# Parking the weight sums of eighteen seven-product units of the down projection in HBM

## The chip, the core and the metric

The kernel runs on one core of one Trainium2 chip. Its time is the device time of one execution, in microseconds (us). Before the change the median of three runs was 1466.16 us (1465.68 to 1466.25).

## What is computed

One layer of a decoder trunk, 256 tokens of 2048 features, all in float32. An attention part with two branches is followed by a gated feed-forward network with a short convolution:

```python
def conv_ffn(h, w_up, conv_w, conv_b, w_down):
    a, b = jnp.split(h @ w_up, 2, axis=-1)                     # 2048 -> 2 x 5632
    ap = jnp.pad(a, ((0, 0), (CONV_WIDTH - 1, 0), (0, 0)))
    c = conv_b
    for j in range(CONV_WIDTH):                                # width 3
        c = c + conv_w[j] * ap[:, j:j + S]
    return (jax.nn.gelu(c, approximate=True) * b) @ w_down     # 5632 -> 2048
...
h = rms_norm(x, norm_mix_pre)
x = x + rms_norm(hybrid_mixer(h, ...), norm_mix_post)
h = rms_norm(x, norm_ffn_pre)
x = x + rms_norm(conv_ffn(h, ffn_w_up, ffn_conv_w, ffn_conv_b, ffn_w_down), norm_ffn_post)
```

The change concerns the product with `w_down`, the GELU, and the stages in which the change places new work.

## The kernel before

**How a product is made.** TensorE (PE) multiplies float32 in a rounded form, so every weight and every activation is split in a high and a low part, and a product is three matmuls: high·high, high·low, low·high (`mm3`, L175 to L177). A weight chunk is 128 rows of 1024 columns (512 KB). SyncE (SP) loads it into a raw tile (`raw_row`, `wchunk`), ScalarE (ACT) casts the high part (`whi`, L143), VectorE (DVE) subtracts it to get the low part (`wlo`, L144), and then PE uses both (`convert`). There are three raw tiles (`RAW`) and four split tiles (`RING`); two more buffers of a tag `flex` serve either as raw tiles (then five raw, four split) or as one split tile (three raw, five split). In `ffn_up` they are a split tile.

**Stages.** After the mixer come `ffn_up0` (c = 0) and `ffn_up(c)` for c = 1 to 10. Each makes 512 columns of `a` and 512 of `b` from 2 × 8 weight chunks, into the accumulators `ua` and `ub`; eight chunks are called a half stage. Results go through `evac` and `conv_cols`, where the convolution (L1083 to L1085), GELU (L1086 to L1091) and the product with `b` are made on ACT and DVE. The down projection is made in two parts, since the activations of all 5632 features don't fit: after c = 5 the first 24 blocks of 128 rows, for two column halves of 1024 (two calls of `pair_gemm`), and after c = 10 the other 20 blocks, 1024 columns by `pair_gemm` (B) and 1024 by `down`.

**Units.** `pair_gemm` works through units of two row blocks, in the order of a string. A plain unit ("p") has 24 matmuls. A seven-product unit ("s", `seven`) uses a scheme that needs seven block products in place of eight, 21 matmuls, and takes sums of blocks: of activations (`token_sums`) and of weights. For the weight sums GpSimd (POOL) loads the two row blocks, and DVE makes four subtractions of 128x512 (L232 to L235) into the tiles `ta` and `tb`; both, the odd block and half of the even one go through `convert`. `PAIR_ORDER` and `B_ORDER` hold the strings; before there are 4 + 3 + 3 units of this kind.

**Order.** `at(t, f)` puts a small task at a tick, and `tick()` is called after every weight chunk of a stage. A scheduler then puts the instructions of each engine in an order of its own; an engine runs its instructions strictly in that order, and one that waits holds all behind it. A tile that is to be reused is waited for by the next writer: a load on POOL into a tile waits until what read the tile before, a store among others, is done.

**Around the change.** At the start of `ffn_up` stand the residual sum and the norm (`resid`, `x2_norm`, `norm_row`): DVE writes a `row` per token tile (L1099), PE spreads it (`rrow`, L1101), and all activations of the stage are scaled with it. POOL stores the residual stream to HBM there (`park`, x_d).

Of the kernel before, what the change touches and what calls it, by code (L numbers as in the profile page):

```python
# [19 lines left out]
P = 128  # L20
D = 2048
# [17 lines left out]
GELU_C = math.sqrt(2.0 / math.pi)  # L39


def trunk_layer(ctx, tc, x, x_cols_in, conv_cols_in, g_mix_post, g_ffn_post, w_in, w_q, w_kv,
# [104 lines left out]
    def raw_row(src):  # L147
        i = cnt[0]
        cnt[0] += 1
        raw = ring_tile("raw", f"raw{i}", F32, in_turn("raw"))  # L150
        nc.sync.dma_start(raw, src)
        return raw
# [52 lines left out]
    def pair_gemm(name, w, k0, c0, order, act_of, s_of, kind, d, place, sums):  # L205
# [17 lines left out]

        def seven(u, last):
# [5 lines left out]
            lo_, hi_ = slice(0, 512), slice(512, 1024)  # L230
            w_ = convert(odd, 1024)
            vec.tensor_tensor(ta[:, lo_], even[:, hi_], even[:, lo_], op=ALU.subtract)  # L232
            vec.tensor_tensor(ta[:, hi_], odd[:, hi_], even[:, hi_], op=ALU.subtract)
            vec.tensor_tensor(tb[:, lo_], odd[:, hi_], ta[:, lo_], op=ALU.subtract)
            vec.tensor_tensor(tb[:, hi_], odd[:, lo_], tb[:, lo_], op=ALU.subtract)  # L235
# [15 lines left out]
            if last:  # L251
                d0, d1, d2, d3 = d() if callable(d) else d

                def first_sums():
                    act.copy(d0, q1)
                    vec.tensor_tensor(d1, d0, q6, op=ALU.add)
                    vec.tensor_tensor(d2, d1, q7, op=ALU.add)

                def more_sums():
                    vec.tensor_tensor(d3, d2, q5, op=ALU.add)  # L260
                    vec.tensor_tensor(d1, d1, q5, op=ALU.add)

                at(now[0], first_sums)
                at(now[0] + 1, more_sums)
# [3 lines left out]
        for i, kd_ in enumerate(order):  # L268
            if kd_ == "s":
                u = next(seven_of)  # L270
                seven(u, u == n - 1)
            else:
                plain(next(plain_of), i == len(order) - 1)
# [466 lines left out]
    tb[1], tb[2] = gate_pair(1)  # L740
    esg.close()
# [145 lines left out]
    b = now[0] + 26  # L887
# [190 lines left out]
    def conv_cols(k, a, b, slot):  # L1078
# [7 lines left out]
        act.activation(uu, cc, AF.Square)  # L1086
        vec.tensor_scalar(uu, uu, 0.044715, 1.0, op0=ALU.mult, op1=ALU.add)
        vec.tensor_tensor(uu, uu, cc, op=ALU.mult)
# [80 lines left out]

    def g_sums(u):  # L1170

        if u % 2 == 0:
            s_tiles.append(sb(p3, [P, D], f"s_{u // 2}", F32R, tag=f"x2_{u // 2}"))
# [45 lines left out]
    es7 = ffn_up0()  # L1219
    for c in range(1, 6):  # L1220
# [3 lines left out]
        if c == 4:  # L1224
            for u in range(4):
                at(now[0] + 3 + 3 * u, lambda u=u: g_sums(u))
        ffn_up(c, 4 * c)
# [6 lines left out]
    sevens_done = [0]  # L1234

    def down_place():
        sevens_done[0] += 1
        i = sevens_done[0]
        if i % 2:
            both = sb(p6, [P, D], f"rr{i}", tag="gp")  # L1240
            return both[:, 0:1024], both[:, 1024:2048]
        return [sb(p6, [P, 1024], f"rr{i}{n}", tag="f" + n, bufs=2) for n in "ab"]

    def f_sums():
        return [sb(p6, [P, 1024], f"t{n}{cnt[0]}", tag="f" + n, bufs=2) for n in "ab"]

    for p in range(2):
        d = [dsum[t][2 * p + j] for t in range(NT) for j in range(2)]
        c = pair_gemm(f"d{p}", w_down, 0, 1024 * p, PAIR_ORDER[p], lambda k, t: (GH(k)[:, t * P:(t + 1) * P], GL(k)[:, t * P:(t + 1) * P]),
                      lambda u: s_of[u], p, d, down_place, f_sums)  # L1250
# [7 lines left out]
    def b_sums(u):  # L1258

        if u % 2 == 0:  # L1260
            sb_tiles.append(sb(p3, [P, D], f"sb_{u // 2}", F32R, tag=f"x2_{u // 2}"))
# [3 lines left out]

    for c in range(6, 11):
        if c == 9:
            for u in range(B_ORDER.count("s")):
                at(now[0] + 10 + 4 * u, lambda u=u: b_sums(u))
# [4 lines left out]
    def z_block(acc, b, t):  # L1274
# [7 lines left out]
        vec.tensor_tensor(zo, z, gpost2[:, c0:c0 + n], op=ALU.mult)  # L1282
# [26 lines left out]
    b_done = [0]  # L1309

    def a_tiles(i, *n):
        return [sb(base, [P, 1024], f"dt{i}_{k}", tag=f"ahl{k}") for k in n]

    def b_place():
        b_done[0] += 1
        return a_tiles(b_done[0], *((0, 1) if b_done[0] % 2 else (4, 5)))
# [3 lines left out]
    def ud_tiles():  # L1320
        ud[:] = [x_[:, j * 512:(j + 1) * 512] for x_ in a_tiles(9, 4, 5) for j in range(2)]
        return ud

    def pair_end(i):
# [3 lines left out]

    c_db = pair_gemm("db", w_down, 24, 0, B_ORDER, lambda k, t: (GH(k)[:, t * P:(t + 1) * P], GL(k)[:, t * P:(t + 1) * P]),
                     lambda u: sb_of[u], 0, ud_tiles, b_place, lambda: a_tiles(20 + b_done[0], *((2, 3) if b_done[0] % 2 else (6, 7))))  # L1330
# [34 lines left out]
B_ORDER = "pppsppspsp"  # L1365
W_ORDER = "ppspspsp"
PAIR_ORDER = ("psppsppsppsp", "ppsppsppsppp")
# [74 lines left out]
```

## Time and profile before

| | |
|---|---|
| median of three runs | 1466.16 us |
| the profiled execution | 1466.82 us |
| its span | 1464.7 us |
| PE busy | 1454.3 us, 99% |
| DVE busy | 1088.9 us, 74% |
| ACT busy | 837.7 us, 57% |
| POOL busy | 70.2 us, 5% |
| moved by DMA | 287.6 MB, 196 GB/s on average |

The profiled execution is 2.1 us longer than its span, which goes from the first to the last instruction that the trace holds. PE, DVE, ACT and POOL are the engines; SP only starts transfers. A row of a timeline has start, duration, engine, line, operation, output<-inputs, and shape. In the windows, each engine's busy time is followed by its number of instructions, and the last three columns are PE's clock, the busy share of the DMA engines, and GB/s. Matmul durations overlap, so the pitch of starts is what a matmul costs.

### The profile page before, as it was taken

How to read it: one execution, taken by the hardware profiler on the slowest of the kernel's cores; microseconds unless marked ns; L12 is line 12 of the kernel's file. 1: busy time of each engine (PE TensorE's matmuls, PEld its weight loads, DVE VectorE, ACT ScalarE, POOL GpSimd, SP SyncE). 2: the span in 40 equal slices, each digit the busy share in tenths (PEclk: the TensorE clock that was granted, in tenths of full speed). 3: DMA queues.
4: the chain of work that ended last, by engine and by line, in shares of the span. 5: the costliest groups of instructions: out<-in, count | busy, mean ns of one | idle time of the engine just before them, and what ended most of it. 6: DMA issues, size and time to landing. Idle time of an engine off the chain costs nothing.

```text
span 1464.7 us, 20974 instructions
## 1 busy us (share of the span) xinstructions
PE 1454.3 (99%) x7567; PEld 1242.8 (85%) x7567; DVE 1088.9 (74%) x1925; ACT 837.7 (57%) x1382; POOL 70.2 (5%) x123
## 2 busy tenths in 40 slices
PE   9999999999999999999999999999999999999997
PEld 7888888888888888888888888888888888888886
DVE  7788896645667665768799976778786687677776
ACT  7588874544555554445666655555454565565553
POOL 0012110000000001000000000000000000000000
PEclk9999999999999999999999999999999999999999
DMA  8755376477655559755766666665656666667573
GB/s 296 216 164 168 105 261 197 160 212 199 188 159 159 165 162 337 263 186 173 235 206 179 199 188 187 191 187 185 206 192 207 201 186 191 186 196 232 163 234 136
DMA packets 147605, 287.60 MB, mean 196 GB/s; under 512 B 18428, under 2 KB 29597, under 8 KB 147373
## 3 DMA queue, kind: packets, MB, share of 16 engines
q1 hardware_dynamic: 137824, 252.60, 56.2%
q0 software_dynamic: 9584, 33.61, 7.3%
q8 instruction: 59, 0.97, 0.3%
q14 instruction: 46, 0.37, 0.1%
q10 hardware_dynamic: 92, 0.05, 0.0%
HBM read 277.79 MB, written 8.44 MB: 195 GB/s over the span
## 4 chain that ended last, share of the span: by engine, by line
PE 94%; DVE 2%; issue 2%; ACT 1%; DMA 1%; POOL 0%; DVEq 0%; ACTq 0%; POOLq 0%
PE accg L175 12%; PE accg L177 12%; PE accg L176 12%; PE ua L1185 10%; PE ub L1185 10%; PE ua L1189 5%; PE ub L1189 5%; PE cd L177 2%; PE cd L175 2%; PE cd L176 2%; PE mpo L875 1%; PE cg L175 1%; PE cw L177 1%; PE cg L177 1%; PE cw L176 1%
## 5 line engine op out<-in xcount | busy, mean ns | idle before, releaser
L144 DVE TENSOR_TENSOR wlo<-raw,whi 128x1024 fp32r<-128x1024 f32 (+2 forms) x470 | 568.4, 1214 | 248.2 <-ACT whi L143 241.2
L143 ACT CAST whi<-raw 128x1024 fp32r<-128x1024 f32 (+2 forms) x470 | 487.9, 1043 | 405.0 <-PE accg L177 156.9
L175 PE MATMUL accg<-whi,ahl 128*128 128x512 f32 (+1 forms) x416 | 162.8, 391 | 0.0
L177 PE MATMUL accg<-whi,ahl 128*128 128x512 f32 (+1 forms) x416 | 160.6, 386 | 0.0
L176 PE MATMUL accg<-wlo,ahl 128*128 128x512 f32 (+1 forms) x416 | 159.8, 384 | 0.0
L1185 PE MATMUL ub<-ahl,whi 128*128 128x512 f32 x640 | 154.6, 391 | 0.0
L1185 PE MATMUL ua<-ahl,whi 128*128 128x512 f32 x640 | 154.6, 391 | 0.0
L175 PE MATMUL accg<-whi,bhl 128*128 128x512 f32 x378 | 148.1, 392 | 0.0
L177 PE MATMUL accg<-whi,bhl 128*128 128x512 f32 x378 | 147.4, 390 | 0.0
L176 PE MATMUL accg<-wlo,bhl 128*128 128x512 f32 x378 | 147.3, 390 | 0.0
L1185 PEld LDWEIGHTS ub<-ahl,whi 128*128 128x128 f32 x640 | 117.5, 188 | 22.9 <-ACT cc L1083 0.3
L1185 PEld LDWEIGHTS ua<-ahl,whi 128*128 128x128 f32 x640 | 117.5, 188 | 22.7
L177 PEld LDWEIGHTS accg<-whi,ahl 128*128 128x128 f32 x416 | 78.1, 188 | 15.4
L176 PEld LDWEIGHTS accg<-wlo,ahl 128*128 128x128 f32 x416 | 78.2, 188 | 13.1
L175 PEld LDWEIGHTS accg<-whi,ahl 128*128 128x128 f32 x416 | 78.2, 188 | 13.0
L1189 PEld LDWEIGHTS ub<-ahl,wlo 128*128 128x128 f32 x640 | 82.2, 191 | 3.2
L1189 PEld LDWEIGHTS ua<-ahl,wlo 128*128 128x128 f32 x640 | 82.2, 191 | 3.1
L1189 PE MATMUL ua<-ahl,wlo 128*128 128x256 f32 x640 | 83.7, 283 | 0.0
L177 PEld LDWEIGHTS accg<-whi,bhl 128*128 128x128 f32 x378 | 71.0, 188 | 14.8
L175 PEld LDWEIGHTS accg<-whi,bhl 128*128 128x128 f32 x378 | 71.0, 188 | 14.4
L1189 PE MATMUL ub<-ahl,wlo 128*128 128x256 f32 x640 | 83.2, 283 | 0.0
L176 PEld LDWEIGHTS accg<-wlo,bhl 128*128 128x128 f32 x378 | 71.0, 188 | 14.3
(616 smaller groups left out, 2376.7 us busy)
## 6 DMA issues: line engine op xcount, KB each, us to landing
raw<-in_ffn_w_up_dram SPq DMA_DIRECT2D x176, 512.0 KB, 4.5
raw<-in_w_in_dram SPq DMA_DIRECT2D x105, 512.0 KB, 4.5
raw<-in_ffn_w_down_dram SPq DMA_DIRECT2D x68, 512.0 KB, 4.6
raw<-in_w_o_swa_dram SPq DMA_DIRECT2D x32, 512.0 KB, 4.0
raw<-in_w_o_mla_dram SPq DMA_DIRECT2D x32, 512.0 KB, 5.4
raw<-in_w_out_dram SPq DMA_DIRECT2D x26, 512.0 KB, 4.5
bias<-strip POOLq DMA_DIRECT2D x16, 256.0 KB, 4.3
raw<-in_mla_w_q_up_dram SPq DMA_DIRECT2D x32, 128.0 KB, 2.5
```

The costliest lines, as they stand in the source:

```text
L143: act.copy(hi[:, a:b], raw[:, a:b])
L144: vec.tensor_tensor(lo[:, a:b], raw[:, a:b], hi[:, a:b].bitcast(F32), op=ALU.subtract)
L175: pe.matmul(o, ah, bh, start=start, stop=False)
L176: pe.matmul(o, ah, bl, start=False, stop=False)
L177: pe.matmul(o, al, bh, start=False, stop=stop)
L875: pe.matmul(o, w(t), p_[:, c], start=n == 0, stop=n == 5)
L1185: pe.matmul(acc[i], hi[:, c], hn[p][:, j * 512:(j + 1) * 512], start=p + j == 0, stop=stop)
L1189: pe.matmul(acc[i][:, 0:256], lo[:, c], hn[p][:, j * 512:j * 512 + 256], start=False, stop=False)
```

## The change

The weight sums of a seven-product unit are no longer made beside the unit. `park_sums` loads the two row blocks of w_down on POOL's queue into one tile, DVE makes the four subtractions in place (now L217 to L220), and POOL stores the two sums to tiles in HBM (L235 and L240). The down projection then reads them back like weights (`seven_parked`, on SP). The subtractions are the same four; a switch puts the halves of the second sum in the other order.

```diff
+    def park_sums(name, w, k, c0, pl, tag, t0, bufs=None):
+
+        td = [dram.tile([P, 1024], F32, name=f"{name}{i}") for i in range(2)]
+        st = []
+
+        def load(i):
+            if i == 0:
+                st.append(sb(pl, [P, D], f"{name}s", tag=tag, bufs=bufs))
+            pool.dma_start(st[0][:, i * 1024:(i + 1) * 1024], w[(k + i) * P:(k + i + 1) * P, c0:c0 + 1024])
+
+        def make():
+            even, odd = (st[0][:, i * 1024:(i + 1) * 1024] for i in range(2))
+            weight_sums(even, odd, even, odd, True)
+            pool.dma_start(td[0], even)
+
+        at(t0, lambda: load(0))
+        at(t0 + 1, lambda: load(1))
+        at(t0 + 3, make)
+        at(t0 + 4, lambda: pool.dma_start(td[1], st[0][:, 1024:2048]))
+        return td
...
+        def seven_parked(u, last):
...
+            w_ = convert(raw_row(row(2 * u + 1)), 1024)
+            mul(c11, act_of(2 * u + 1, 0), half(w_, 0))
+            mul(c12, s4, half(w_, 1))
+            w_ = convert(raw_row(row(2 * u)[:, 0:512], 512), 512)
+            mul(q1, act_of(2 * u, 0), half(w_, 0), last)
+            w_ = convert(raw_row(parked[u][0]), 1024)
...
+            w_ = convert(raw_row(parked[u][1]), 1024)
...
-B_ORDER = "pppsppspsp"
+B_ORDER = "psspsspssp"
-PAIR_ORDER = ("psppsppsppsp", "ppsppsppsppp")
+PAIR_ORDER = ("ppspspsspssp", "ppspspsspssp")
+EARLY = 4
```

With the strings there are 6 + 6 + 6 units. The sums of twelve are parked for the first part of the down projection and of six for B. Four of the twelve (`EARLY`) are made in the gate and output stages of the attention part, in a tile with two buffers; the other eight from `ffn_up0` on, and the six of B from c = 6 on, all in one buffer of the tag "gp":

```diff
+    parked_a = [park_a(i, pg, "gr", now[0] + 6 * i, bufs=2) for i in range(EARLY)]
+    out_b(1, tb[1], (pss, "s"))
+    tb[3] = gate_b(3)
+    out_b(2, tb[2])
     esg.close()
...
-    b = now[0] + 26
+    b = now[0] + 2
...
-    for j in range(1, 4):
-        out_b(j, tb[j], (pss, "s") if j == 1 else None)
-        if j == 1:
-            tb[3] = gate_b(3)
+    out_b(3, tb[3])
...
     es7 = ffn_up0()
+    for i in range(2 * NA - EARLY):
+        parked_a.append(park_a(i + EARLY, p6, "gp", now[0] + 16 + 6 * i))
...
+    parked_b = [park_sums(f"tb{i}_", w_down, 24 + 2 * i, 0, p6, "gp", now[0] + 4 + 6 * i) for i in range(NB_)]
```

Three stages of the attention part (`out_b(1)`, `gate_b(3)`, `out_b(2)`) are thus written ahead of the multi-head latent attention and not inside it. The down projection has more raw tiles: `more_raw` gives seven in turn, three of the ring and four that are idle then. GELU has one DVE instruction less, and the gain of the last norm is loaded into two tiles just before B (before, after the first part):

```diff
-        act.activation(uu, cc, AF.Square)
-        vec.tensor_scalar(uu, uu, 0.044715, 1.0, op0=ALU.mult, op1=ALU.add)
-        vec.tensor_tensor(uu, uu, cc, op=ALU.mult)
+        act.activation(uu, cc, AF.Square, scale=GELU_R)
+        vec.scalar_tensor_tensor(uu, uu, 1.0, cc, op0=ALU.add, op1=ALU.mult)
...
+    def deep_raws():
+        turn_flex("w")
+        more_raw[:] = [raw_of, f_raw("a"), raw_of, f_raw("b"), raw_of, f_raw("a"), f_raw("b")]
+
+    turn_flex("raw")
+    at(now[0] + 8, deep_raws)
...
-    gpost2 = sb(p6, [P, D], "gpost2", tag="gp")
-    pool.dma_start(gpost2, g_ffn_post.partition_broadcast(P))
...
+    gpost2 = [a_tile(f"gpost2_{i}", i) for i in range(2)]
+    for i in range(2):
+        pool.dma_start(gpost2[i], g_ffn_post[1024 * i:1024 * (i + 1)].partition_broadcast(P))
```

**Where the instructions stand now.** The first place is DVE in `ffn_up(3)`, where before the weight subtractions of four chunks follow each other (`ua`, `f` and `bhl` are accumulators and activations of the stage, the numbers count tiles):

```order
L144 TENSOR_TENSOR wlo_8901<-raw_8898,whi_8900 128x1024 [waits DMAHW3_49,PE_49,Activation_49]
L318 TENSOR_TENSOR bhl_7609<-uu_8921,bhl_7609 128x256 [waits Activation_49]
L144 TENSOR_TENSOR wlo_8949<-raw_8946,whi_8948 128x1024 [waits DMAHW4_49,Activation_49]
L144 TENSOR_TENSOR wlo_8971<-raw_8968,whi_8970 128x1024 [waits DMAHW5_49,PE_49,Activation_49]
L144 TENSOR_TENSOR wlo_8993<-raw_8990,whi_8992 128x1024 [waits DMAHW6_49,Activation_49]
L144 TENSOR_TENSOR wlo_9015<-raw_9012,whi_9014 128x1024 [waits DMAHW7_49,PE_49,Activation_49]
L1207 SCALAR_TENSOR_TENSOR f_3_8933<-ua_0_8701,f_3_8933 128x256 [waits Activation_49]
```

The row of `f` that follows is the evacuation of `ua`. With the change the same stretch begins with the last subtraction of the eleventh parked unit and holds the first of the twelfth (`ta_s` is the shared tile, `sa` and `sm` are sums of activations for a seven-product unit):

```order
L220 TENSOR_TENSOR ta_s<-ta_s 128x512 [waits DVE_49]
L340 TENSOR_TENSOR sa_9832<-bhl_7652 128x512
L145 TENSOR_TENSOR wlo_9033<-raw_9030,whi_9032 128x1024 [waits DMAHW4_49,Activation_49]
L343 TENSOR_TENSOR sm_9833<-sa_9832 128x128 [waits DVE_49]
L344 TENSOR_TENSOR sm_9833<-sa_9832 128x128
L345 TENSOR_TENSOR sm_9833<-sm_9833,sa_9832 128x128 [waits DVE_49]
L145 TENSOR_TENSOR wlo_9057<-raw_9054,whi_9056 128x1024 [waits DMAHW5_49,PE_49,Activation_49]
L346 TENSOR_TENSOR sm_9833<-sa_9832,sm_9833 128x128 [waits DVE_49]
L340 TENSOR_TENSOR sa_9988<-bhl_7653 128x512 [waits DVE_49]
L145 TENSOR_TENSOR wlo_9080<-raw_9077,whi_9079 128x1024 [waits DMAHW6_49,Activation_49]
L217 TENSOR_TENSOR ta_s<-ta_s 128x512 [waits DMASW5_49,DMASW4_49,DMASW3_49]
L145 TENSOR_TENSOR wlo_9102<-raw_9099,whi_9101 128x1024 [waits DMAHW7_49,PE_49,Activation_49]
```

Between L220 and L217 stand three weight chunks and six sums of activations. L217 waits for three transfers (DMASW are semaphores of POOL's queue), and the next weight chunk stands behind it.

The second place is POOL. Before, two loads for the first seven-product unit stand between the stores of the residual stream, and then nothing until the down projection:

```order
L1160 DMA x_d<-x_0_5851 128x512 x4
L227 DMA rr_10082<-in_ffn_w_down_dram 128x1024
L228 DMA rr_10082<-in_ffn_w_down_dram 128x1024
L1160 DMA x_d<-x_1_5852 128x512 x4
L227 DMA rr2a<-in_ffn_w_down_dram 128x1024
```

With the change POOL goes round this from the fifth parked unit on (L230 loads the row blocks, L235 and L240 store the sums; here the ninth and the tenth unit):

```order
L230 DMA ta_s<-in_ffn_w_down_dram 128x1024 [waits DMASW7_49,DMASW0_49]
L230 DMA ta_s<-in_ffn_w_down_dram 128x1024
L235 DMA ta_0_7850<-ta_s 128x1024 [waits DMASW1_49,DVE_49]
L240 DMA ta_1_7851<-ta_s 128x1024 [waits DMASW2_49,DVE_49]
L230 DMA ta_s<-in_ffn_w_down_dram 128x1024 [waits DMASW4_49,DMASW3_49]
L230 DMA ta_s<-in_ffn_w_down_dram 128x1024
L235 DMA ta_0_7852<-ta_s 128x1024 [waits DMASW5_49,DVE_49]
L240 DMA ta_1_7853<-ta_s 128x1024 [waits DMASW6_49,DVE_49]
```

Each load into the shared tile stands behind the stores of the unit before and waits for them.

The third place is the start of the second product of `ffn_up0`. On DVE, before, the `row` of the second token tile (L1099) stands ahead of three weight chunks:

```order
L1019 TENSOR_SCALAR rfh_7594<-rf_y 128x1
L1099 TENSOR_SCALAR row<-ident,rf_y 128x128
L144 TENSOR_TENSOR wlo_7647<-raw_7644,whi_7646 128x1024
L144 TENSOR_TENSOR wlo_7670<-raw_7667,whi_7669 128x1024
L144 TENSOR_TENSOR wlo_7693<-raw_7690,whi_7692 128x1024
L1111 TENSOR_TENSOR hx_7662<-hx_7662,row 128x512
```

With the change (L1161 is now the line of `row`, L1082 and L361 to L373 belong to the norm) the fifth parked unit's four subtractions stand in the norm, ahead of these rows, and the chunks stand between the two rows:

```order
L145 TENSOR_TENSOR wlo_7691<-raw_7688,whi_7690 128x1024
L1082 TENSOR_SCALAR rfh_7614<-rf_y 128x1
L361 SCALAR_TENSOR_TENSOR rf_t<-vh_7624,rf_y 128x1
L1161 TENSOR_SCALAR row<-ident,rf_y 128x128
L371 TENSOR_SCALAR rf_u<-rf_t 128x1
L145 TENSOR_TENSOR wlo_7714<-raw_7711,whi_7713 128x1024
L372 TENSOR_TENSOR rf_u<-rf_u,rf_t 128x1
L145 TENSOR_TENSOR wlo_7737<-raw_7734,whi_7736 128x1024
L373 SCALAR_TENSOR_TENSOR rf_y<-rf_u,rf_y 128x1
L1082 TENSOR_SCALAR rfh_7638<-rf_y 128x1
L1161 TENSOR_SCALAR row<-ident,rf_y 128x128
L145 TENSOR_TENSOR wlo_7755<-raw_7752,whi_7754 128x1024
```

The second L1161, of the second token tile, now stands behind three weight chunks. On PE the product with the rows stood ahead of the second product's first matmul (accg_0_7624):

```order
L176 MATMUL accg_1_7403<-wlo_7491,bhl_6580 128x512
L177 MATMUL accg_1_7403<-whi_7490,bhl_6580 128x512 [waits DVE_49]
L1101 MATMUL rrow<-row,ones_p 128x256 [waits DVE_49]
L175 MATMUL accg_0_7624<-whi_7628,bhl_6573 128x512
L176 MATMUL accg_0_7624<-wlo_7629,bhl_6573 128x512
```

With the change (now L1163) it stands inside that product:

```order
L184 MATMUL accg_0_7668<-whi_7672,bhl_6617 128x512
L185 MATMUL accg_0_7668<-wlo_7673,bhl_6617 128x512
L1163 MATMUL rrow<-row,ones_p 128x256 [waits DVE_49]
L186 MATMUL accg_0_7668<-whi_7672,bhl_6617 128x512
L184 MATMUL accg_1_7669<-whi_7672,bhl_6617 128x512
```

It is now reached eight matmuls later.

More of the change, by code (lines that the diff above doesn't have):

```diff
@@ L270, in pair_gemm @@
                 u = next(seven_of)
-                seven(u, u == n - 1)
+                (seven_parked if parked else seven)(u, u == n - 1)
             else:
@@ L1226, in trunk_layer @@
                 at(now[0] + 3 + 3 * u, lambda u=u: g_sums(u))
+        if c == 5:
+            for u in range(4, NA):
+                at(now[0] + 3 + 5 * (u - 4), lambda u=u: g_sums(u))
         ffn_up(c, 4 * c)
@@ L1232, in down, with turn_flex @@
         return gemm(xh, xl, w_down, k0, nk, c0, n, split=split, ps=ps)
[L1234 to L1245, printed above, removed]
+    def turn_flex(kind):
+        flex[0] = kind
+        turn.update(raw=0, w=0)
+    f_raw = lambda n: lambda name: sb(p6, [P, 1024], name, tag="f" + n, bufs=2)
+    def deep_raws():
[3 more added lines that the diff above has]
+    at(now[0] + 8, deep_raws)
     for p in range(2):
@@ L1264, in b_sums @@
         sb_of[u] = token_sums(gtiles[u].bitcast(F32), a, m, hi, lo)
+    parked_b = [park_sums(f"tb{i}_", w_down, 24 + 2 * i, 0, p6, "gp", now[0] + 4 + 6 * i) for i in range(NB_)]
     for c in range(6, 11):
         if c == 9:
[L1268 to L1269 removed]
+            for u in range(NB_):
+                at(now[0] + 2 + 4 * u, lambda u=u: b_sums(u))
         ffn_up(c, 4 * (c - 6))
```

95 lines of the change are left out of this document (64 added, 31 removed).

## The prediction

> **What bounds the kernel now.** I read the page's busy shares and chain first, then PE's waits, then the rows of VectorE, and last the DMA rows.
>
> ```profile
> span 1464.7 us, 20974 instructions
> PE 1454.3 (99%) x7567; PEld 1242.8 (85%) x7567; DVE 1088.9 (74%) x1925; ACT 837.7 (57%) x1382; POOL 70.2 (5%) x123
> ...
> DVE  7788896645667665768799976778786687677776
> ...
> PE 94%; DVE 2%; issue 2%; ACT 1%; DMA 1%; POOL 0%; DVEq 0%; ACTq 0%; POOLq 0%
> ```
>
> ```profile
> PE warm L77 <- DVE ramp L66: 1.1, 1, 1.1
> PE pstrip L349 <- DMA sel<-in_strip_sel_dram: 0.8, 1, 0.8
> PE cdb L176 <- DVE wlo L144: 0.2, 1, 0.2
> ```
>
> PE is busy 99% of the span and waits 2.1 us in all, so the time is the number of matmuls times their pitch. Fewer matmuls pay in full; a wait that reaches PE costs in full. Every weight chunk has to pass DMA, a cast on ACT and a subtraction on DVE before PE can use it, so what matters of the other engines is whether they stay ahead.
>
> **The gain.** The timeline of PE in the down projection holds one matmul per row; 45 steps lie between these two starts.
>
> ```profile
> 1014.74 0.39 PE L176 MATMUL cd<-wlo,bhl 128*128 128x512 f32 x1
> ...
> 1024.94 0.39 PE L176 MATMUL qd<-wlo,s 128*128 128x512 f32 x1
> ```
>
> (1024.94 − 1014.74) / 45 = 0.2267 us (the 0.39 of a row is a modelled duration that overlaps the next). A seven-product unit has 21 matmuls where a plain one has 24, and eight units change: 24 × 0.2267 = **−5.44 us**. All of it lies on PE's path.
>
> **What the change adds to VectorE.** Rows of the groups by form, and the line of a weight sum:
>
> ```profile
> L144 DVE TENSOR_TENSOR wlo<-raw,whi 128x1024 fp32r<-128x1024 f32 x458 | 558.7, 1224 | 246.2 <-ACT whi L143 239.3 <-PE ub L1185 3.0 <-PE ua L1185 2.5
> L1088 DVE TENSOR_TENSOR uu<-uu,cc 128x256 f32<-128x256 f32 x44 | 18.3, 419 | 0.3
> L1087 DVE TENSOR_SCALAR uu<-uu 128x256 f32<-128x256 f32 x44 | 12.2, 287 | 0.7 <-ACT uu L1086 0.5
> L551 DVE TENSOR_TENSOR p<-s,bias 128x128 f32<-128x128 f32 x32 | 9.2, 286 | 6.4 <-PE s L549 6.4
> L1008 DVE SCALAR_TENSOR_TENSOR bhl<-x2T,gmat,bhl 128x128 fp32r<-128x128 f32 x32 | 9.1, 342 | 0.8 <-ACT bhl L1005 0.6
> ```
>
> ```profile
> L232 DVE TENSOR_TENSOR ta<-rr x4: 684/688/692, 977.4 to 1085.9; 128x512 f32<-128x512 f32 x4
> ```
>
> A parked unit takes four subtractions of 0.685 us, 2.74 us, away from the down projection, where they stood beside their unit, and puts them earlier; 18 × 2.74 = 49 us of DVE are moved or added. GELU loses 44 × 0.287 = 12.6 us (the page counts 12.2 busy). None of this is on PE's path as long as DVE stays ahead, and in the down projection DVE gets lighter, so I cost it at nothing there. The first four parks lie in slices in which DVE is busy 4 to 6 tenths, and their tile is double: nothing. The other fourteen lie in ffn_up, one tile after the other. There the cover is thin:
>
> ```profile
> 778.30:800.60 22.30, 22.30 (x138) 19.93 (x137) 19.78 (x38) 13.43 (x24) 0.00 (x0) 1.00 0.62 188
> ...
> 889.60:911.90 22.30, 22.30 (x130) 19.70 (x129) 17.03 (x30) 13.40 (x23) 0.00 (x0) 1.00 0.66 189
> sum 133.60, PE 133.60 PEld 118.10 DVE 107.91 ACT 80.15 POOL 0.00; mean PE 22.27 PEld 19.68 DVE 17.99 ACT 13.36 POOL 0.00
> ```
>
> Six half stages of c = 1 to 3: DVE is idle 133.6 − 107.9 = 25.7 us, and the seven parks there take 19.2 of it. At 189 GB/s a chunk of 524 kB comes every 2.78 us, which is PE's pace.
>
> **The wait that it adds.** The parks of ffn_up share one tile. After a park's last subtraction (L220) its second sum is stored, then the next two row blocks are loaded, and only then can the next L217 start. L217 stands in DVE's order, and behind it stand the weight subtractions that PE needs. No row of before shows this chain; its parts have neighbours:
>
> ```profile
> raw<-in_ffn_w_up_dram SPq DMA_DIRECT2D x176, 512.0 KB, 4.5
> ...
> rr<-in_ffn_w_down_dram POOLq DMA_DIRECT2D x8, 512.0 KB, 4.5
> ...
> yb_d<-tb POOLq DMA_DIRECT2D x8, 256.0 KB, 3.9
> ...
> ta_d<-ta POOLq DMA_DIRECT2D x8, 256.0 KB, 4.9
> ...
> x_d<-x POOLq DMA_DIRECT2D x8, 256.0 KB, 6.1
> ...
> mr<-in_w_out_dram POOLq DMA_DIRECT2D x2, 512.0 KB, 7.4
> ```
>
> A load of the same rows on the same queue lands in 4.5 us; a store of half the size in 3.9, 4.9 or 6.1. I take 4.9 + 4.5, and 0.5 for two hand-overs to POOL: a chain of 9.9 us. Its lower bound is 3.9 + 3.9 + 0.5 = 8.3 (a load as fast as the fastest store), its upper 6.1 + 4.9 + 0.5 = 11.5.
>
> In that time DVE does what its order puts between L220 and the next L217. Counted there and priced with the rows above (1.224 for a weight chunk, 0.685, 0.42, 0.285 for 512, 256, 128 columns), the work from the sixth park to the twelfth is 7.9, 13.2, 8.1, 10.6, 9.1 and 6.2 us. Instructions overlap a little: seven of L1008 take 1.89 us in the timeline, where 7 × 0.342 would be 2.39, so some 0.08 less each; the work is then 6.8, 11.2, 7.1, 9.3, 8.0 and 5.5.
>
> ```profile
> 741.92 1.89 DVE L1008 SCALAR_TENSOR_TENSOR bhl<-x2T,gmat,bhl 128x128 fp32r<-128x128 f32 x7
> ```
>
> Against 9.9 the waits are 2.0 + 0 + 1.8 + 0 + 0.8 + 3.7 = 8.3 us by full durations, and 3.1 + 0 + 2.8 + 0.6 + 1.9 + 4.4 = 12.8 with the overlap: I take the middle, 10.6. For the six parks of c = 6 to 8 the first gap holds only three chunks at PE's pace (8.3 us, wait 1.6); the other four hold 8.1, 5.9, 8.5 and 9.3 us of work, or 7.1, 5.2, 7.4 and 8.1: waits of 1.8 + 4.0 + 1.4 + 0.6 = 7.8, or 2.8 + 4.7 + 2.5 + 1.8 = 11.8. With the first, the middle is 11.4.
>
> What covers a wait is DVE's lead. The five split-weight tiles let it work four chunks ahead: 4 × 2.78, less a cast and a subtraction (1.05 + 1.22), is 8.9 us. But DVE's own bursts use part of it already:
>
> ```profile
> L143 ACT CAST whi<-raw 128x1024 fp32r<-128x1024 f32 (+2 forms) x470 | 487.9, 1043 | 405.0 <-PE accg L177 156.9
> ```
> ```profile
> 798.10 1.22 DVE L144 TENSOR_TENSOR wlo<-raw,whi 128x1024 fp32r<-128x1024 f32 x1
> 802.42 1.21 DVE L144 TENSOR_TENSOR wlo<-raw,whi 128x1024 fp32r<-128x1024 f32 x1
> 806.85 2.36 DVE L144 TENSOR_TENSOR wlo<-raw,whi 128x1024 fp32r<-128x1024 f32 x2
> ```
>
> Two chunks take 8.75 us there instead of 5.56, so 3.2 of the lead is spoken for, and 5.7 is left. With DVE nearly full while the parks run, it is not won back between two of them, only in c = 4 and 5. So PE waits 10.6 − 5.7 = 4.9 us in the first group and 11.4 − 5.7 = 5.7 in the second: **+10.6 us** (6.3 by full durations, 14.9 with the overlap).
>
> [...]
>
> **One more wait at the start of ffn_up's second product.** The fifth park now stands in the code between residual and norm, so four subtractions and three weight chunks are ahead of the scale row of the second token tile.
>
> ```profile
> 750.65 0.28 DVE L1099 TENSOR_SCALAR row<-ident,rf_y 128x128 f32<-128x128 f32 x1
> 751.37 3.95 DVE L144 TENSOR_TENSOR wlo<-raw,whi 128x1024 fp32r<-128x1024 f32 x3 [0.44 <-ACT whi L143]
> ```
> ```profile
> 754.17 0.59 PE L1101 MATMUL rrow<-row,ones_p 128*128 128x256 f32 x2
> ```
>
> The row comes at 750.65 + 4 × 0.6 + 3.95 = 757.0, 0.28 later it is done, and 0.44 is won as DVE no longer waits for the cast: 756.8. PE reaches the product of the row eight matmuls later than before, at 754.17 + 1.81 = 755.98. **+0.9 us** (0 to 3).
>
> **The other edits.** Three stages are written before the attention pool opens instead of in it; the order around them keeps its place, and DVE is far from full there: nothing. The down projection reads the parked sums through SP: its first stage has twelve units of 3.5 row blocks and twelve of two, 66 × 524 kB = 34.6 MB in 540 × 0.2267 = 122 us. That is 283 GB/s, where before shows 194, but more has been moved:
>
> ```profile
> 575.00:580.00 5.00, 5.00 (x26) 4.17 (x25) 3.57 (x5) 1.67 (x3) 1.08 (x2) 1.00 1.05 390
> ...
> 1000.60:1126.00 125.40, 125.40 (x555) 103.88 (x554) 97.05 (x114) 63.70 (x74) 6.33 (x12) 1.00 0.61 194
> ```
>
> With seven raw tiles instead of three or five I cost it at nothing: 72 loads in 122 us are 1.70 us each, and seven of these less a cast and a subtraction cover a landing of 9.6 us. Above that it could be 5 us. The post-norm gain comes in two halves just before the last product, which is 222 × 0.2267 = 50 us ahead of its use: nothing.
>
> **The sum.** −5.44 + 0.9 + 10.6 = +6.1. The profiled execution took 1466.82 (span 1464.7 and 2.1 around it), 0.66 above the median of the runs, 1466.16. So 1472.9 against the profiled one, **1472.2 us** as median.
>
> **Rivals.**
> Faster: the chain is short. At 8.3 us every gap loses 1.6: waits of 4.1 and 3.8, both inside the lead, so 1466.16 − 5.44 + 0.9 = **1461.6**. For it: pairs of loads on an idle queue. It decides below a chain of about 9.0, where PE's waits are 2.4. Against it: the store is twice the size of the rows that I have, beside SP's stream. 0.22.
> The same: the chain near 9.3, and PE loses 3 to 8 us: about **1466**. 0.16.
> Much slower: SP's stream suffers. Park traffic is 2.1 MB in about 14 us, 150 GB/s on top of 189. With three raw tiles a chunk cycle is landing + 1.05 + 1.22 + 0.1; three chunks take 8.34 us, so a landing above 6.0 us slows every chunk. At the 7.4 us of the row of mr it is 3.26 us per chunk, 0.48 × 44 chunks = 21 us, less the lead of 5.7, and the same for part of the second group: with the chain of 11.5 (PE's waits of 12.9 + 13.7 = 26.6) about **1488**. [...] 0.17.
> The down projection is short of data, the ffn_up waits staying in the lead: 1461.6 + 5 = **1466.6**. 0.05.
> The forecast: 0.40.
>
> **How the numbers follow.** Faster by over 0.2% (2.9 us, about what a measurement of this kernel can tell from no change) is below 1463.2: the short chain, 0.22, and a little of the rest: 0.23. The same, 1463.2 to 1469.1: 0.16 + 0.05 less what falls outside, 0.17. Slower: 0.60. The forecast's own range is 1467.9 to 1476.5 by the two ways of counting; the range reaches to the other cases, 1461.2 to 1488.
>
> **What would show it.** Right: PE's waits name weight chunks of ua and ub, in c = 1 to 3 and 6 to 8, and DVE's idle time has L217 waiting for its load, some 20 us in all; the landings of the sums' stores are about 5 us. Wrong: L217 never waits, or landings of ffn_up's weights pass 6 us, or PE's waits lie in the down projection.

## The result and the profile after

The changed kernel takes 1491.58 us (median of 6 runs, 1484.54 to 1495.08) against 1466.49 for the kernel before on the same chips (6 runs, 1465.68 to 1467.51): a ratio of 1.0163 [1.0136, 1.0189], 25.1 us slower. The forecast was 1472.2 with a range up to 1488.0: the direction was right, and the time lies 3.6 us above the range. The profiled execution took 1491.42 us, so the trace is a typical one.

The page of the changed kernel, its span, its busy shares and the engines' shares of the chain that ended last:

```profile
span 1489.6 us, 21276 instructions
PE 1458.3 (98%) x7543; PEld 1242.0 (83%) x7543; DVE 1119.7 (75%) x1959; ACT 851.2 (57%) x1403; POOL 98.6 (7%) x176
...
PE 78%; DMA 10%; DVE 6%; issue 4%; ACT 2%; POOL 0%; DVEq 0%; SPq 0%; ACTq 0%; POOLq 0%
```

There are 24 matmul records fewer, and yet PE is busy 4.0 us longer and idle 20.9 us longer. The chain was PE for 94% before and is now 78%: DMA and DVE took most of the rest. The three longest sums of PE's waits in the changed kernel (us in all, times, longest us):

```profile
PE ub L1254 <- DVE wlo L145: 12.7, 7, 5.3
PE ub L1250 <- DVE uu L1153: 4.7, 2, 4.0
PE ua L1254 <- DVE wlo L145: 2.4, 3, 1.3
```

These three are 19.8 us, all of them in ffn_up, and none was there before (a wait of 0.6 us for a row of GELU makes it 20.4). DVE is late with weight chunks (`wlo`), and also with rows of GELU (`uu`), which the prediction had not named. What DVE itself waited for at the first subtraction of a parked unit (L217, of which the sums of the first part of the down projection are `ta_s` and those of B `tb_s`):

```profile
DVE ta_s L217 <- DMA ta_s<-in_ffn_w_down_dram: 15.9, 4, 7.5
DVE tb_s L217 <- DMA tb_s<-in_ffn_w_down_dram: 15.0, 3, 6.9
DVE ta_s L217 <- issue: 9.4, 3, 5.4
...
DVE tb_s L217 <- issue: 7.6, 2, 4.2
```

Together 47.9 us. Of the first row 11.2 us fall on the early four units (before 336 us); 36.7 us are left for ffn_up, 14.1 of them in c = 1 to 3 and 22.6 in c = 6 to 8. The rows that end in "issue" name no releaser, but the timeline shows that they are the same wait. DVE and POOL of the changed kernel round one hand-over of the shared tile:

```profile
792.12 0.68 DVE L220 TENSOR_TENSOR ta_s<-ta_s 128x512 f32<-128x512 f32 x1
...
805.22 0.69 DVE L217 TENSOR_TENSOR ta_s<-ta_s 128x512 f32<-128x512 f32 x1 [5.39 <-issue]
```
```profile
793.09 0.54 POOL L240 DMA_DIRECT2D ta<-ta_s  x1 [2.92 <-DVE ta_s L220]
798.92 1.06 POOL L230 DMA_DIRECT2D ta_s<-in_ffn_w_down_dram  x2 [5.29 <-DMA ta<-ta_s]
```

L220 ends at 792.80, POOL issues the store at 793.09, waits 5.29 us for it, issues the two loads from 798.92 on, and L217 starts at 805.22: a chain of 12.4 us where I took 9.9. DVE stands still for 5.39 us of it, with GELU's next row behind L217. At the nine hand-overs of ffn_up at which L217 waited, the chain took 10.2 to 14.7 us, with a median of 11.7: 0.3 to the issue of the store, 5.2 (4.0 to 6.9) from there to the issue of the loads, 6.3 (5.3 to 7.5) from there to L217. The landings of the changed kernel, KB each and median us:

```profile
raw<-in_ffn_w_up_dram SPq DMA_DIRECT2D x176, 512.0 KB, 4.6
...
ta_s<-in_ffn_w_down_dram POOLq DMA_DIRECT2D x24, 512.0 KB, 6.2
ta<-ta_s POOLq DMA_DIRECT2D x24, 512.0 KB, 4.5
tb_s<-in_ffn_w_down_dram POOLq DMA_DIRECT2D x12, 512.0 KB, 7.0
tb<-tb_s POOLq DMA_DIRECT2D x12, 512.0 KB, 4.9
```

The stores are about what I took (4.9), the loads are not (4.5 taken, 6.2 and 7.0 measured). Windows of the changed kernel by stage: c = 1 to 5, the first down projection, c = 6 to 10 (length; busy PE, PEld, DVE, ACT, POOL; granted PE clock, DMA share, GB/s):

```profile
778.00:1015.00 237.00, 227.96 (x1299) 199.75 (x1298) 189.01 (x322) 132.99 (x218) 13.88 (x26) 0.99 0.76 245
1015.00:1137.00 122.00, 122.00 (x540) 101.06 (x539) 91.08 (x99) 73.60 (x84) 1.06 (x2) 1.00 0.81 271
1137.00:1377.00 240.00, 228.63 (x1285) 200.66 (x1284) 177.97 (x293) 126.46 (x201) 12.81 (x24) 0.98 0.74 236
```

The first down projection moves 271 GB/s, and PE never waits in it. Most of the loss lies in the two groups of ffn_up: PE is idle 9.0 and 11.4 us there. They grew by more than that, and the clock column gives a part of the reason: 0.99 and 0.98 in place of 1.00. Lengths in us, each from the first matmul of a stage to the first of the next, as the timeline of PE gives them (the first from the span's start, the last to the start of the last matmul); "none", "traffic" and "no wait" are e_rest, e_traf and e_nowait below, whose profiled executions took 1462.1, 1467.2 and 1476.0 us (that of e_traf is 3.0 us below the median of its runs):

| stretch | before | after | none | traffic | no wait |
|---|---|---|---|---|---|
| start to c = 1 | 776.4 | 778.5 | 776.1 | 775.9 | 778.3 |
| c = 1 to 5 | 224.5 | 236.7 | 225.2 | 230.3 | 234.4 |
| first down projection | 125.8 | 122.4 | 122.4 | 122.4 | 122.4 |
| c = 6 to 10 | 222.7 | 239.3 | 222.7 | 223.9 | 226.3 |
| second down projection | 107.2 | 104.7 | 105.5 | 104.7 | 104.7 |

The two down projections give back 3.4 + 2.5 = 5.9 us, 2.1 are lost ahead of c = 1, and ffn_up costs 12.2 + 16.6 = 28.8. Of these PE stands idle for 20.4; 8.4 lie in time that counts as busy. Windows put 5.4 of the 8.4 down to PE's clock: it is granted at 0.50 from 807.32 to 810.73, from 1182.78 to 1189.61 and from 1220.33 to 1223.74, and half of the 10.7 us in which PE is busy there is lost. Some 2 us more are waiting that counts as busy, since each of PE's 13 waits is counted from the modelled end of the matmul before it, 0.39 us long where the pitch of starts is 0.227, so 0.16 us too late. The last 1 us is not explained. The slow clock followed stalls of 3.98, 5.28 and 3.43 us. The second of them, PE's timeline and a window behind it:

```profile
1178.31 1.11 PE L1254 MATMUL ub<-ahl,wlo 128*128 128x256 f32 x8
1184.71 2.07 PE L1254 MATMUL ub<-ahl,wlo 128*128 128x256 f32 x8 [5.28 <-DVE wlo L145]
1186.58 3.41 PE L1250 MATMUL ub<-ahl,whi 128*128 128x512 f32 x8
```
```profile
1185.00:1190.00 5.00, 5.00 (x17) 4.28 (x17) 5.00 (x10) 2.82 (x4) 0.54 (x1) 0.54 0.96 313
```

After a wait of 5.28 us the granted clock is 0.54 in the window from 1185 to 1190: 5.00 × 0.46 = 2.3 us more are lost in matmuls that count as busy.

### The profile page after: what moved, and what is told of

Same layout as the page of the kernel before. It is cut to its first block, busy times and chain, and to the rows that moved or that the text cites. A ratio compares the mean times of both kernels' runs of the same rounds, so it can differ in the third digit from the quotient of the medians.

```text
span 1489.6 us, 21276 instructions
## 1 busy us (share of the span) xinstructions
PE 1458.3 (98%) x7543; PEld 1242.0 (83%) x7543; DVE 1119.7 (75%) x1959; ACT 851.2 (57%) x1403; POOL 98.6 (7%) x176
## 4 chain that ended last, share of the span: by engine, by line
PE 78%; DMA 10%; DVE 6%; issue 4%; ACT 2%; POOL 0%; DVEq 0%; SPq 0%; ACTq 0%; POOLq 0%
PE accg L184 11%; PE accg L186 11%; PE accg L185 11%; PE ub L1250 7%; PE ua L1250 6%; PE ub L1254 4%; PE ua L1254 3%; DMA raw<-in_ffn_w_up_dram 3%; DVE wlo L145 3%; DMA tb_s<-in_ffn_w_down_dram 2%; PE cd L185 2%; PE cd L184 2%; PE cd L186 2%; DMA tb<-tb_s 2%; DMA ta_s<-in_ffn_w_down_dram 1%
## 5 line engine op out<-in xcount | busy, mean ns | idle before, releaser
L145 DVE TENSOR_TENSOR wlo<-raw,whi 128x1024 fp32r<-128x1024 f32 (+2 forms) x526 | 625.1, 1197 | 219.6 <-ACT whi L144 214.7
L144 ACT CAST whi<-raw 128x1024 fp32r<-128x1024 f32 (+2 forms) x526 | 537.6, 1028 | 431.6 <-PE accg L186 158.6
L1250 PE MATMUL ub<-ahl,whi 128*128 128x512 f32 x640 | 157.8, 396 | 4.7 <-DVE uu L1153 4.7
L1254 PE MATMUL ub<-ahl,wlo 128*128 128x256 f32 x640 | 87.0, 288 | 12.7 <-DVE wlo L145 12.7
L185 PEld LDWEIGHTS accg<-wlo,ahl 128*128 128x128 f32 x416 | 78.2, 188 | 14.1 <-DVE wlo L145 1.0
```

The source lines that it names most:

```text
L144: act.copy(hi[:, a:b], raw[:, a:b])
L145: vec.tensor_tensor(lo[:, a:b], raw[:, a:b], hi[:, a:b].bitcast(F32), op=ALU.subtract)
L185: pe.matmul(o, ah, bl, start=False, stop=False)
L1250: pe.matmul(acc[i], hi[:, c], hn[p][:, j * 512:(j + 1) * 512], start=p + j == 0, stop=stop)
L1254: pe.matmul(acc[i][:, 0:256], lo[:, c], hn[p][:, j * 512:j * 512 + 256], start=False, stop=False)
```

## The experiments

Two theories: **the chain** (L217 waits in DVE's order for its tile, as forecast) and **the traffic** (park loads and stores make SP's stream late, which the prediction had as a rival). The texts set down ahead of the runs weigh a third, **the work** (DVE has too much to do with the moved subtractions). All ratios are against the kernel before, with 95% intervals.

**1. The waits taken away, the transfers kept** (e_nowait). From the sixth unit on the subtractions work on a scratch tile that nothing loads. (The scratch tile is set to zero once on DVE, and since it takes the place of a tile of `g_sums`, two of those sums of c = 4 stand eight chunks later.)

```
-            weight_sums(even, odd, even, odd, True)
...
+                x, y = (scratch[0][0][:, i * 1024:(i + 1) * 1024] for i in range(2))
+                weight_sums(x, y, x, y, True)
...
```

> From the sixth parked unit on, DVE's four subtractions work on a scratch tile and no longer wait for the load; loads and stores run as in the change, and the stored blocks are the loaded ones, so the sums are left out. Chain theory (DVE waits at L217 for store and load through one tile): no waits there, PE waits only in the early units and at the scale row, 1466.5 - 5.4 + 2 to 4 = 1463 to 1465. Traffic theory (parks slow SP's weight loads): the same bytes, even denser, so still near 1490. Work theory (DVE overfull): the same subtractions, still 1485 or more.

1477.43 us, 1.0072 [1.0054, 1.0091]. The time lies between what the chain theory gave (1463 to 1465) and what the other two gave (1485 and more). The waits cost 1491.6 − 1477.4 = **14.2 us**, and 10.9 more than the kernel before is left without them: the chain is not the whole.

**2. No parking** (e_rest). The down projection reads rows of the weights in place of the kept sums; everything else of the change stays.

```
-        td = [dram.tile([P, 1024], F32, name=f"{name}{i}") for i in range(2)]
...
+        return [w[(k + i) * P:(k + i + 1) * P, c0:c0 + 1024] for i in range(2)]
```

> All of the change but the parking: no loads, sums or stores ahead of time, and the eighteen units read plain rows of w_down where the sums would be (so the sums are left out). What the change could bring if parking cost nothing: 1466.5 - 5.9 = 1460 to 1461 by every theory. If it is slower, another edit (stages moved, raw tiles, GELU) costs something.

1461.68 us, 0.9965 [0.9951, 0.9979]: the eight more units of seven products, the moved stages and SP's larger stream together give 4.8 us of the 5.44 forecast, so the other edits cost at most some 0.6.

**3. The subtractions alone** (e_work). As e_rest, and DVE does the eighteen times four subtractions on a tile that nothing loads or stores.

```
...
+            x, y = (scr[key][:, i * 1024:(i + 1) * 1024] for i in range(2))
+            weight_sums(x, y, x, y, True)
...
+        return [w[(k + i) * P:(k + i + 1) * P, c0:c0 + 1024] for i in range(2)]
```

> As e_rest, with the four subtractions of each parked unit on DVE, on a tile that nothing loads, and no transfer. Chain theory: only the place at the start of ffn_up costs, up to 6 us: 1461 to 1467. Work theory: the stalls left in e_nowait are work, so 1470 to 1478. Traffic theory: 1461 to 1464.

1461.74 us, 0.9967 [0.9954, 0.998]. DVE has the time: 0.1 us. That rules the work out as a cause by itself.

**4. The transfers alone** (e_traf): loads and stores as in the change, no subtractions.

```
-            weight_sums(even, odd, even, odd, True)
+            pass
```

> As the change, all loads and stores, but no subtraction, so DVE never waits for a transfer of POOL's (the stored blocks are the loaded ones). Chain theory: 1461 to 1464. Traffic theory, by what is left in e_nowait: 1470 to 1478. Work theory: 1461 to 1463.

1470.14 us, 1.0025 [1.0013, 1.0038] (1467.0 to 1475.3): **8.5 us** over e_rest for traffic that nobody waits for at L217. What ACT waited for before its casts, in e_rest and then in e_traf:

```profile
ACT whi L144 <- DMA raw<-in_ffn_w_up_dram: 21.1, 16, 2.1
```
```profile
ACT whi L144 <- DMA raw<-in_ffn_w_up_dram: 100.5, 67, 5.1
```

The casts wait five times as long for ffn_up's weights (17.0 us in the kernel before, 105.1 in the changed one), although the median landing rose only from 4.5 to 4.6. The late landings do not show in it: for the 55 loads of c = 1 to 3 (775 to 930 us) the landings, least, median and longest, were in e_rest and then in e_traf

```profile
DMA to landing us min/median/max: 3.6/4.5/6.2
```
```profile
DMA to landing us min/median/max: 3.6/4.6/9.4
```

PE's longest wait in e_traf shows how a late landing gets to it, through a row of GELU that stands on ACT behind a late cast. ACT and then PE in e_traf:

```profile
786.45 1.05 ACT L144 CAST whi<-raw 128x1024 fp32r<-128x1024 f32 x1 [5.14 <-DMA raw<-in_ffn_w_up_dram]
787.40 0.56 ACT L1146 ACTIVATE cc<-fT,cvT 128x256 f32<-128x256 f32 x1
```
```profile
793.58 0.63 PE L1192 MATMUL fT<-ident,f 128*128 128x128 f32 x4 [2.69 <-DVE uu L1153]
```

SP itself issued no load between 782.60 and 788.79 there: it went on when DVE had subtracted that chunk (at 788.76) and its raw tile was free. With three raw tiles one late landing held up the next loads too, here for 6.2 us.

**5. Deeper landing buffers under that traffic** (e_trafraw). As e_traf, and the two spare tiles, which ffn_up uses for split weights, are raw tiles there: five raw and four split in place of three and five.

```
+    turn_flex("raw")
     for i in range(2 * NA - EARLY):
...
```

> As e_traf (all loads and stores of the parking, no subtraction, so the sums are left out), with five raw tiles in ffn_up for three. If the 8.5 us of e_traf are SP's loads landing late behind the park traffic with too few raw tiles: 1461 to 1464. If they are anything else of the traffic (a slower store, a write to HBM beside PE): still 1468 to 1472.

1466.00 us, 0.9997 [0.9987, 1.0006], between the two forecasts: 4.1 of the 8.5 us are gone. In the profiled run c = 1 to 5 takes 225.6 us, as in e_rest. What is left is one stall where the spare tiles change hands at c = 6, in PE's timeline of e_trafraw:

```profile
1126.95 2.00 PE L1250 MATMUL ua<-ahl,whi 128*128 128x512 f32 x8
1131.32 3.47 PE L1250 MATMUL ua<-ahl,whi 128*128 128x512 f32 x8 [2.37 <-ACT whi L144]
```

**6. The same buffers under the change as it is** (e_fonly): the diff of 5, with the subtractions.

> The change with nothing but the spare tiles as raw tiles in ffn_up. The wait of DVE at L217 stays (chain of 12 us), and the lead that covers it is 2.8 us shorter; late landings no longer cost. Chain and traffic theory together: 1491.6 less the 8.5 of e_traf, plus some of the shorter lead, 1483 to 1490. Traffic theory alone: 1462 to 1466.

1493.65 us, 1.0194 [1.0172, 1.0215]: no help, and above the 1483 to 1490 that both theories together gave. DVE's waits in it:

```profile
DVE ta_s L217 <- DMA ta_s<-in_ffn_w_down_dram: 22.2, 6, 6.4
DVE tb_s L217 <- DMA tb_s<-in_ffn_w_down_dram: 16.3, 4, 6.5
DVE ta_s L217 <- issue: 7.5, 3, 3.5
...
DVE tb_s L217 <- issue: 1.9, 1, 1.9
```

That is 47.9 us, as in the changed kernel: more room for SP's stream did not shorten the chain on POOL's queue.

**7. L217 tied to a later place** (e_late). A one-column instruction of DVE makes L217 depend on the latest weight chunk, so that it cannot stand early in DVE's order, and the units of ffn_up start every eight chunks (the early four have the tie too, and start every five).

```
+            vec.scalar_tensor_tensor(even[:, 0:1], last_lo[0][:, 0:1].bitcast(F32), 0.0, even[:, 0:1], op0=ALU.mult, op1=ALU.add)
             weight_sums(even, odd, even, odd, True)
...
-        at(t0 + 3, make)
+        at(t0 + late, make)
...
-        parked_a.append(park_a(i + EARLY, p6, "gp", now[0] + 16 + 6 * i))
+        parked_a.append(park_a(i + EARLY, p6, "gp", now[0] + 2 + 8 * i))
...
```

> One tile as before, but units every 8 chunks, and the first subtraction tied behind a weight chunk (a one-element operation reads it), so that 7 chunks (19 us) lie between two units. Chain theory: the chain of about 12 us is covered, no wait at L217, 1462 to 1464. Traffic theory: the same bytes over a longer time, so part of the loss stays, 1470 to 1480. Work theory: DVE's load is spread as well, 1462 to 1466.

1467.95 us, 1.0008 [0.9995, 1.002], between the forecasts of the chain and the traffic theory. The wait at the first instruction of a unit (now L235), the only one of its kind left in e_late, and ACT's wait for weights:

```profile
DVE ta_s L235 <- DMA ta_s<-in_ffn_w_down_dram: 0.3, 1, 0.3
```
```profile
ACT whi L145 <- DMA raw<-in_ffn_w_up_dram: 130.7, 91, 5.9
```

The chain is hidden, the traffic is not: the time is close to that of the traffic alone (1470.1). The transfers are spread over more time (the loads of the fifth to the twelfth unit start within 211 us here, within 100 in e_traf), but that this makes them cheaper is not clear of the noise. In the profiled execution, the slowest of the ten, 4.1 us of the loss lie in the first down projection (126.5 us where the changed kernel has 122.4); a cast of ACT waits 5.8 us for a load of `w_down` there.

**8. The same tie, every four chunks** (e_gap4): `now[0] + 2 + 4 * i` and `late=3`.

> As the version with units every 8 chunks, but every 4, so that 3 to 5 chunks (8 to 14 us) lie between the end of one unit and the next. Chain theory: against a chain of 12 us waits of about 3 us at most of the 12 units, 36 us, less two leads of 5.7: PE loses 20 to 30 and the time is 1480 to 1495. Traffic theory: as dense as the change, 1485 to 1495. Work theory: as the change, 1485 to 1495.

1498.07 us, 1.0219 [1.0201, 1.0236], 3 us above all three forecasts. DVE's waits in e_gap4:

```profile
DVE tb_s L235 <- DMA tb_s<-in_ffn_w_down_dram: 20.6, 5, 6.3
DVE ta_s L235 <- DMA ta_s<-in_ffn_w_down_dram: 19.4, 5, 8.1
```

Four chunks at PE's pace are 4 × 2.78 = 11.1 us, a unit's own subtractions included, less than the chain (median 11.7 in the changed kernel) without them, and 40 us of waits are back. The distance decides, not the tie.

**9. Two tiles in turn** (e_two): every other unit uses a second tile, so that its loads need not wait for the stores of the unit before. (Two of the `g_sums` of c = 4 stand eight chunks later, as in experiment 1.)

```
-        parked_a.append(park_a(i + EARLY, p6, "gp", now[0] + 16 + 6 * i))
+        parked_a.append(park_a(i + EARLY, *((p3, "x2_1") if i % 2 else (p6, "gp")), now[0] + 16 + 6 * i + 2 * (i % 2)))
...
```

> Two tiles in turn for the units in ffn_up; the order packs the units closer, four chunks between two uses of one tile. Chain theory: a chain of 12 us against 11 us and more of work, waits of about 1 us at a few units, inside the lead: 1463 to 1472. Traffic theory: denser traffic than in the change, 1491 or more. Work theory: 1490 or more, since the same work stands in fewer chunks.

1487.96 us, 1.0136 [1.012, 1.0153]: a miss. The scheduler used the freedom to put eight units into 40 chunks where they had taken 51. One of the landings and DVE's waits in e_two:

```profile
tb_s<-in_ffn_w_down_dram POOLq DMA_DIRECT2D x12, 512.0 KB, 8.5
```
```profile
DVE ta_s L217 <- DMA ta_s<-in_ffn_w_down_dram: 14.2, 6, 7.3
DVE tb_s L217 <- DMA tb_s<-in_ffn_w_down_dram: 13.6, 4, 6.2
```

The loads of the second group take 8.5 us where they had 7.0 (those of the first 6.2 as before), and L217 waits for them again. Two tiles at an unchanged distance were not tried, so what the tile itself costs stays open.

**10 to 12. Both remedies** (e_best, e_flex, e_flex2). e_best is e_late with seven chunks between the units of the first group; e_flex adds the five raw tiles of experiment 5; e_flex2 is e_flex with the spare tiles handed over four chunks later at c = 6.

```
-        parked_a.append(park_a(i + EARLY, p6, "gp", now[0] + 2 + 8 * i))
+        parked_a.append(park_a(i + EARLY, p6, "gp", now[0] + 2 + 7 * i))
```
```
...
+    turn_flex("raw")
...
-    turn_flex("raw")
+    at(now[0] + 4, lambda: turn_flex("raw"))
```

> As e_late, but units every 7 chunks ahead of the first part of the down projection, so that the last store is over some chunks before the activation sums reuse the tile (in e_late a cast on ACT waited 6 us for it, and PE lost 3 behind it). Chain theory: 1460.6 and some 2 us of short stalls beside loads: 1462 to 1465. Traffic theory: as e_late, 1466 to 1469.

> As e_best (units 7 and 8 chunks apart, tied behind a weight chunk), and the two spare tiles serve as raw tiles in ffn_up: five raw and four split tiles for three and five. If what is left beside the chain is SP's loads landing late behind the park traffic, five raw tiles cover a landing of 5 x 2.78 - 2.4 = 11.5 us and the loss goes: 1461.5 to 1464. If it is DVE's own lead, which is one chunk shorter here, it gets worse: 1471 to 1480.

> As e_flex, with the spare tiles given to the raw ring 4 chunks into c = 6 and not right after the down projection's first part (in e_flex PE waits 1.6 us there for a cast whose raw tile comes late). That wait goes: 1460 to 1462, against 1462.0 of e_flex; if the spare tiles are needed for the first parked unit of this group, no gain or 1462 to 1465.

e_best 1470.76 us, 1.0035 [1.0021, 1.0048], no better than e_late and above what both theories gave. e_flex **1462.02 us, 0.9974 [0.9964, 0.9984]**, faster than both kernels and 0.3 us above e_rest. e_flex2 1462.33 us, 0.9971 [0.9959, 0.9982], not to be told from e_flex: the gain expected does not show. All of PE's waits in e_flex:

```profile
PE ua L1252 <- ACT whi L145: 1.6, 1, 1.6
PE warm L78 <- DVE ramp L67: 1.1, 1, 1.1
PE acckv L479 <- ACT whi L145: 0.4, 1, 0.4
```

e_flex keeps all eighteen units' loads, stores and subtractions; only their times, their place in DVE's order and the landing buffers differ from the changed kernel.

## Why the prediction was wrong

In medians the time adds up in steps:

| step | us | against the step before |
|---|---|---|
| before | 1466.5 | |
| more units, no parking (e_rest) | 1461.7 | −4.8 |
| subtractions alone (e_work) | 1461.7 | +0.1 |
| transfers alone (e_traf) | 1470.1 | +8.5 over e_rest |
| both, without the waits from the sixth unit on (e_nowait) | 1477.4 | +7.3 |
| with them: the change | 1491.6 | +14.2 |

The steps are sizes in this order and not fixed prices: without the waits at L217 the transfers follow each other faster. The loads of the fifth to the twelfth unit start within 166 us in the change, within 108 in e_nowait and 100 in e_traf. That the waits and the traffic are what costs, and nothing else, rests on e_flex, which keeps all loads, stores and subtractions and ends 0.3 us above e_rest.

**The gain** was right: −5.44 forecast, −4.8 measured in e_rest, −5.9 by the stages of the changed kernel. **Nothing for DVE's added work** was right (0.1 us), and so, within some 0.6 us, was nothing for the moved stages and the down projection's data.

**The wait** was the right mechanism in the right place, c = 1 to 3 and 6 to 8, but under-sized. DVE's waits there were forecast as 10.6 + 11.4 = 22.0 us and are 14.1 + 22.6 = 36.7. The term that was mis-sized is the load in the chain: I priced it at 4.5 us by `rr`, a load of the same rows elsewhere in the program; in the loop of the shared tile loads took 6.2 and 7.0 in the median, and the chain 11.7 where 9.9 was taken. Even the upper bound of 11.5 had only 4.9 for the load, although the row of `mr` showed a load of 7.4 us on the same queue. In time the waits cost 14.2 us by e_nowait where I had +10.6 (6.3 to 14.9), so this step alone would have left the forecast inside its range.

**The traffic** is the step that failed. "SP's stream suffers" stood as a rival with 0.17, and the forecast held nothing of it; it is 8.5 us by itself. I had made it depend on landings above 6.0 us and read that off the median; the median stayed at 4.6, and yet ACT waited 100.5 us in place of 21.1. What the median leaves out are the late landings beside a park, 9.4 us at the longest where e_rest has 6.2, and with three raw tiles a late landing held up the next loads too (in e_traf SP issued none from 782.60 to 788.79 us). In experiment 5 two more raw tiles took half of the cost away (4.1 of 8.5 us). Whether the loads or the stores of the parking make SP's loads late was not separated.

**The cover.** The forecast added its terms as if each had the lead of the weights to itself. Transfers and subtractions cost 8.5 and 0.1 apart and 15.7 together (1477.4 − 1461.7), 7.1 more than their sum. Some 2 us of this are the early four units, whose waits (10.4 us on DVE in e_nowait, 11.2 in the change) I had called nothing: the table of stretches has 778.3 and 778.5 there against 775.9. (It varies: e_fonly, with the same early code, has 776.0.) In the profiled executions most of the rest is one stall, at the place of that of experiment 4. In e_nowait PE waits 5.8 us there for a row of GELU (`fT`, 2.7 in e_traf), and the half clock behind it lasts 6.8 us in place of 3.4. A lead that late weights and subtractions both draw on would do this, but no run shows that apart. In the changed kernel itself the cover was no thinner than forecast: DVE waited 14.1 and 22.6 us, PE stood idle 9.0 and 11.4, so 5.1 and 11.2 us were covered where I had subtracted 5.7 and 5.7.

**The stall's price.** PE's waits were counted once. In the changed kernel 20.4 us of idle time in ffn_up brought 5.4 us with them that were lost at half clock. Nothing in the trace of before shows this: PE's longest wait there was 1.1 us.

**The row of the scale** was over-sized: 0.9 forecast (0 to 3), about 0.1 found. From the start of the row's product to the second matmul behind it 0.76 us pass in the changed kernel (757.92 to 758.68) and 0.67 passed before (754.17 to 754.84).

The criterion "PE's waits name weight chunks" held for 15.1 of the 19.8 us; the rest, 4.7, are GELU's rows, which stand in DVE's order behind L217 just as the chunks do. I had looked only for chunks there. None of the three signs of being wrong showed: L217 did wait, the median landing stayed below 6 us, and PE did not wait in the down projection. The second was the sign for the step that failed, and it was asked of the wrong quantity.

## What to carry to other kernels

The transfers that "run beside" this kernel had two prices, and the trace of before shows neither: the wait of their consumer (14.2 us by e_nowait), which the place of that instruction in DVE's order sets, and the delay of the stream beside them (8.5 us by e_traf, 4.1 of them gone with two more landing buffers). Here either remedy alone left nothing of the gain (1468.0 with the consumer later, 1493.7 with more buffers), and both together brought the whole gain. Load-work-store loops through one tile should be laid out at the measured turnaround (10.2 to 14.7 us here, some four to five chunks) plus a margin, and for the stream beside them one should look at how long its consumer waits, not at the median landing.

## What the runs showed of the hardware

**Half clock followed some of PE's stalls.** In the changed kernel three of the 13 waits in ffn_up were followed by half clock, those of 3.98, 5.28 and 3.43 us; ten waits of 0.2 to 2.5 us were not. The length of the wait alone does not tell them apart: in e_trafraw a wait of 2.37 us (quoted in experiment 5) was followed by half clock, and this one of the changed kernel was not:

```profile
910.70 1.22 PE L1254 MATMUL ub<-ahl,wlo 128*128 128x256 f32 x8 [2.53 <-DVE wlo L145]
```

The stretches of half clock in the changed kernel are 3.41, 6.83 and 3.41 us long, and their starts (807.32, 1182.78, 1220.33) lie 375.46 and 37.55 us apart, 110 and 11 times 3.413. So in this execution all changes of the clock between 20 and 1440 us lie multiples of 3.413 us apart. In windows of that length, in step with the half clock of each run, the two waits differ. First e_trafraw, two windows, then the changed kernel, two windows (the column behind POOL's is the clock):

```profile
1127.48:1130.89 3.41, 1.47 (x7) 0.88 (x5) 0.00 (x0) 0.67 (x1) 0.54 (x1) 1.00 0.94 369
1130.89:1134.31 3.42, 2.99 (x7) 2.43 (x8) 1.69 (x2) 1.93 (x3) 0.00 (x0) 0.50 0.24 60
```
```profile
906.30:909.72 3.42, 1.87 (x13) 1.51 (x11) 0.90 (x2) 1.24 (x2) 0.00 (x0) 1.00 0.99 388
909.72:913.13 3.41, 2.43 (x14) 2.19 (x15) 2.77 (x5) 0.10 (x1) 0.54 (x1) 1.00 0.45 118
```

The wait of 2.37 us left PE idle for 1.94 us of one window, and the next had half the clock. The wait of 2.53 us was divided, 1.55 us in one window and 0.98 in the next, and the clock stayed at 1.00. Cut in this way, the changed kernel has three windows at full clock between 20 and 1440 us in which PE idled for 2.99 to 3.41 us, each with half clock in the next. In all its other windows at full clock it idled for 1.55 us or less, and none of them was followed by half clock. Why the clock changes at these times was not shown.

**The median hid late landings.** With POOL's traffic beside it, the median landing of SP's loads of `w_up` hardly moved (4.5 us in e_rest, 4.6 in e_traf), while the longest one of c = 1 to 3 went from 6.2 to 9.4 us and ACT's waits for these loads from 21.1 to 100.5 us.
